# Softmax remainders' products one step later on TensorE, and eleven weight remainders subtracted on VectorE

## The chip, the cores and the metric

One Trainium2 chip, of which the kernel uses one core. A core has TensorE (PE, matrix products into PSUM banks), VectorE (DVE), ScalarE (ACT), GpSimd (POOL) and SyncE (SP), each with its own queue of instructions, which it works off in order, and DMA queues that move data between device memory and SBUF. The metric is the device time of one execution in microseconds. The median of three executions of the kernel before is 932.94 us (932.41 to 934.12).

## The reference

One transformer layer over 128 context tokens and 512 latent tokens of width 1024: RMSNorm with a modulation, one projection into queries, keys and values of two mixers (A: attention with grouped heads; B: attention in a window of the grid with a bias) and into two gates; the gated merge of both mixers, an output projection, and an MLP.

```
aq, ak, av, bq, bk, bv, ga, gb = split(h @ w_in)
p = softmax(scores);  o = p @ v                      # mixer A: 8 heads; mixer B: 8 heads, window + context
m = sigmoid(ga) * (a_o @ w_br_a) + sigmoid(gb) * (b_o @ w_br_b)
x = x + g1 * (m @ w_out)
x = x + g2 * (square(relu(h2 @ w1)) @ w2)
```

Everything is float32.

## The kernel before

A float32 matrix is split into a part that TensorE takes exactly at its fast rate (`hi`, type fp32r) and the remainder `lo = x - hi`. A product is then three: hi by hi, hi by lo, lo by hi (`gemm_k`, L311 to L313). Features lie on the 128 partitions, tokens run along the free axis, in two halves of 320.

**Attention (55 to 322 us).** The sixteen heads run one after another (`HeadA`, `HeadB`, and a `CtxPair` for the context queries after every second head). While one head makes its scores (L674 and L675 in A, L727 and L728 in B) and their exponentials, the head before it is transposed and multiplied with the values, step by step: `T(t)` transposes the probabilities of one key tile on TensorE into a bank `pt` (L684, L744; two such banks), and `p_split` turns it into `ph` (ScalarE, L622) and the remainder `pl` (VectorE, L623). A step later `pv()` multiplies both with the values into the head's bank `po`, of which there is one: L691 and L692 in A (five steps of 512 columns), L755 and L756 in B (four steps with different widths). `pl` is multiplied directly behind `ph` of the same step. At the last step `combine` takes `po` out. `ph`, `pl`, the `ct` of `combine`, the reciprocals `rc` of a pair of heads and the context's `pc` share five tiles of tag `r`. Between these steps stand the projections of later heads and of the gates as filler.

**Merge (322 to 440 us).** For each of eight output tiles n: two gates (tiles 18 + n and 26 + n of `w_in`, 24 products for each half), their sigmoids on ScalarE, then the products of tile n of `w_br` (12 for each mixer and half), multiplied with the gates on VectorE (L1143), added (L1144) and split into `mh` (ScalarE, L1145) and `ml` (VectorE, L1146). Tiles 21, 29, 22 and 30 are made in attention and come back from device memory as `sg`. The weights come in the order 18, 26, `br` 0, 19, 27, `br` 1, 20, 28, `br` 2, `br` 3, `br` 4, 23, 31, `br` 5, and so on. Beside it VectorE makes the modulation for the second half of the layer from 32 transfers (`wmt`, products `mt`, L1065), in portions between the rest.

`Weights.conv()` prepares a weight: it is loaded into `wst` (three tiles), ScalarE makes `hi` (L263), and the remainder is made in one of three ways. For a weight in `LOSET`, which is built from the table `LOACC`, ScalarE writes -hi into `lo` (L265) and GpSimd's queue starts a transfer that reads the weight a second time and adds it (L266). Otherwise VectorE, or for a few weights GpSimd, subtracts (L272, in two halves for `w_in`). `hi` and `lo` have three tiles each, so a weight is converted when the one three places ahead of it is done.

What sets the order: from the merge until the MLP begins, VectorE runs in the order in which the code is written. All other orders of these stages (TensorE, ScalarE, GpSimd, SyncE, and VectorE in attention) are planned when the program is built, from the dependences.

Of the kernel before, what the change touches and what calls it, by code (L numbers as in the profile page):

```python
# [16 lines left out]
P = 128  # L17
# [35 lines left out]
NST = 3  # L53
NB = 4
NU = 6
BLKPOOL = (("A12", "A22"), ())
AUTO = (0, 0)
LAG3 = 5
# [2 lines left out]
TQ = 2  # L61
P3 = 8
GPV = 1
LOACC = (("in", 21, 22), ("in", 29, 30), ("in", 20, 26), ("in", 27, 34), ("br", 0, 8))
FINP = ()
HALVES = (slice(0, HT), slice(HT, NT))

# [2 lines left out]
def trunk_layer(ctx: ExitStack, tc: tile.TileContext, xT, small_in, wmodA, wmodB, tabs, cacheK, cacheV, bias,  # L70
                w_in, w_br, w_out, w1, w2, yT, akT, avT, bkT, bvT):
    nc = tc.nc
    PE, ACT, DVE = nc.tensor, nc.scalar, nc.vector
# [23 lines left out]
    def open_phase(name, nu):  # L97
        phase.close()
        cur["p"] = phase.enter_context(tc.tile_pool(name=name, bufs=1, reuse_waits="tile"))
        cur["nu"] = nu  # L100
        return cur["p"]
# [7 lines left out]
    def o_tile(name, dt=F32):  # L109
        return hp_.tile([P, NT], dt, tag="o", bufs=9, name=name)  # L110
# [4 lines left out]
    def tt_tile(name):  # L115
        return cur["p"].tile([P, NT], F32R, tag="tt", bufs=12, name=name)
# [4 lines left out]
    def ps_(tag, name):  # L121
        return psum["p"].tile([P, 512], F32, tag=tag, bufs=psum["n"][tag], name=name)
# [10 lines left out]
    def ps_t():  # L133
        return ps_("t", "pt")

    def ps_o():
        return ps_("o", "po")

    def r32(ap):
        return ap.bitcast(F32)  # L140
# [162 lines left out]
    EXTRA = {("out", 4), ("w1", 0)}  # L303
    LOSET = {(x, n) for x, a, b in LOACC for n in range(a, b) if x != "in" or n not in GATES[2:]}
    W = Weights()
# [206 lines left out]
    kp = open_phase("attn", 8)  # L512
# [8 lines left out]
    SHUF = [(i + 16) % 32 for i in range(32)]  # L521

    def r_(name, dt=F32):
        return kp.tile([P, 512], dt, tag="r", bufs=5, name=name)

    def rf(name):
        return kp.tile([P, 512], F32, tag="rf", bufs=2, name=name)
# [33 lines left out]
    def half(e):  # L561
        return slice(64 * e, 64 * e + 64)
# [57 lines left out]
    def p_split(pt, n):  # L620
        ph, pl = r_("ph", F32R), r_("pl", F32R)
        ACT.activation(ph[:, :n], pt[:, :n], AF.Copy)  # L622
        DVE.tensor_sub(pl[:, :n], pt[:, :n], r32(ph[:, :n]))  # L623
        return ph, pl

    def combine(dst, ps, n):

        t = r_("ct")
        ACT.activation(t[0:64, :n], ps[64:P], AF.Copy)
        DVE.tensor_add(dst, ps[0:64], t[0:64, :n])  # L630
# [10 lines left out]
    def pair_sums(mixer, j):  # L641
        RC[mixer, j] = r_("rc")
        sm = SUMS[mixer, j]
        DVE.reciprocal(sm, sm)
        ACT.activation(RC[mixer, j].rearrange("p (q e d) -> p q e d", q=4, e=2),
                       sm.rearrange("p (e q) -> p q e", e=2).unsqueeze(3).broadcast_to([P, 4, 2, 64]), AF.Copy)

    def pair_norm(mixer, j):

        rc, o = RC[mixer, j], (AO if mixer == "a" else BO)[j]  # L650
        rows = ps_t()
        for qt in range(4):
            PE.transpose(rows[:, qt * P:(qt + 1) * P], rc[:, qt * P:(qt + 1) * P], ident)
        DVE.tensor_mul(o[:, P:NT], o[:, P:NT], rows)

    class HeadA:
# [24 lines left out]
        def T(self, t):  # L681
            pt = ps_t()
            for qt in range(4):
                PE.transpose(pt[:, qt * P:(qt + 1) * P], self.p[qt][:, t * P:(t + 1) * P], ident)  # L684
            ph, pl = p_split(pt, 512)

            def pv():
                if t == 0:
                    self.po = ps_o()
                v = AV(t + 1, self.g)  # L690
                PE.matmul(self.po, v, ph, start=(t == 0), stop=False)  # L691
                PE.matmul(self.po, v, pl, start=False, stop=(t == 4))  # L692
                if t == 4:
                    combine(AO[self.j][half(self.e), P:NT], self.po, 512)
                    if self.e:
                        after.append(lambda: pair_norm("a", self.j))
                return 470
            if t == 1 and self.e:
                pair_sums("a", self.j)
            return 520, pv  # L700
# [5 lines left out]
    class HeadB:  # L706
# [31 lines left out]
        def T(self, gi):  # L738
            pt = ps_t()
            c = 0  # L740
            for t, q0, q1 in BG[gi]:
                for qt in range(q0, q1):
                    k = (0, 0, 384, 256)[qt] if t == 4 else (P if qt < 2 else 0) + (t - BL[qt]) * P
                    PE.transpose(pt[:, c:c + P], self.p[qt][:, k:k + P], ident)  # L744
                    c += P
            ph, pl = p_split(pt, c)

            def pv():
                if gi == 0:
                    self.po = ps_o()  # L750
                c = 0
                for t, q0, q1 in BG[gi]:
                    n = (q1 - q0) * P
                    v = BV[self.j](5 if t == 4 else t + 1, self.e)
                    PE.matmul(self.po[:, q0 * P:q1 * P], v, ph[:, c:c + n], start=(gi == 0), stop=False)  # L755
                    PE.matmul(self.po[:, q0 * P:q1 * P], v, pl[:, c:c + n], start=False, stop=(gi == 3))  # L756
                    c += n
                if gi == 3:
                    combine(BO[self.j][half(self.e), P:NT], self.po, 512)
                    if self.e:  # L760
                        after.append(lambda: pair_norm("b", self.j))
                return 440
            if gi == 1 and self.e:
                pair_sums("b", self.j)
            return 420, pv
# [262 lines left out]

    open_phase("late", NU)
    v_pool = ExitStack()  # L1030
# [70 lines left out]
    class Units:  # L1101
        n = 0
# [11 lines left out]
    for j in range(4):  # L1114
        for src, dst in ((AO[j], AOS), (BO[j], BOS)):
            d = (tt_tile("osh"), o_tile("osl", F32R))
# [194 lines left out]
    class Operands:  # L1311
# [38 lines left out]
        def conv(self):  # L1350
# [6 lines left out]
            ACT.activation(w[:, 0:4], t, AF.Copy)  # L1357
            (nc.gpsimd if o in BLKPOOL[l - 1] else DVE).tensor_sub(w[:, 4:8], t, r32(w[:, 0:4]))  # L1358
            if o in ("S3", "S2", "A22"):
# [236 lines left out]
    for x in SEQ:  # L1596
        l, c, n, o = x
        w = OPS[0].get(x)
# [143 lines left out]
```

## Time and profile before

| what | value |
|---|---|
| median of three executions | 932.94 us (932.41 to 934.12) |
| the profiled execution | 933.35 us, of which the span is 931.4 us |
| granted TensorE clock | 0.998 |
| transfers | 151.08 MB; q1 (SP) 33.0% of 16 engines' span, q0 (POOL) 29.7% |
| accumulating transfers `wl<-w_in` | 11, of 512 KB, median 8.0 us from issue to landing |
| stage 430 to 525 us, output projection and norm | PE busy 94.88 of 95.00 us, DVE 74.46 |
| stage 525 to 620 us, MLP | PE 95.00 of 95.00 us, DVE 83.45 |

Times are microseconds from the start of the span, unless ns is written. PEld is TensorE's weight load, which runs beside the product ahead of it. L12 is line 12 of the kernel before. A wait of the form "engine line <- engine line" gives its total, how often it occurred, and the longest.

### The profile page before, as it was taken

How to read it: one execution, taken by the hardware profiler on the slowest of the kernel's cores; microseconds unless marked ns; L12 is line 12 of the kernel's file. 1: busy time of each engine (PE TensorE's matmuls, PEld its weight loads, DVE VectorE, ACT ScalarE, POOL GpSimd, SP SyncE). 2: the span in 40 equal slices, each digit the busy share in tenths (PEclk: the TensorE clock that was granted, in tenths of full speed). 3: DMA queues.
4: the chain of work that ended last, by engine and by line, in shares of the span. 5: the costliest groups of instructions: out<-in, count | busy, mean ns of one | idle time of the engine just before them, and what ended most of it. 6: DMA issues, size and time to landing. Idle time of an engine off the chain costs nothing.

```text
span 931.4 us, 16637 instructions
## 1 busy us (share of the span) xinstructions
PE 913.3 (98%) x6166; PEld 879.2 (94%) x6166; DVE 716.2 (77%) x1491; ACT 566.5 (61%) x1153; POOL 193.3 (21%) x223
## 2 busy tenths in 40 slices
PE   9999999999999999999999999999999999999996
PEld 7799889989999999999999999999999999999995
DVE  5665887756756797486688996986798778985898
ACT  4566777756656765765423577536763576457765
POOL 0020200002201011211130010445233532364130
PEclk9999999999999999999999999999999999999999
DMA  9783310125636479999753362888778887798473
GB/s 348 293 241 107 90 44 26 61 67 143 163 87 159 135 240 263 258 237 269 238 160 114 103 192 77 141 191 190 171 128 191 181 170 158 165 191 175 94 114 113
DMA packets 54032, 151.08 MB, mean 162 GB/s; under 512 B 6656, under 2 KB 10384, under 8 KB 53952
## 3 DMA queue, kind: packets, MB, share of 16 engines
q1 hardware_dynamic: 31440, 100.27, 33.0%
q0 software_dynamic: 21360, 48.45, 29.7%
q10 hardware_dynamic: 1152, 1.31, 0.4%
q8 instruction: 48, 0.79, 0.3%
q14 instruction: 32, 0.26, 0.1%
HBM read 138.72 MB, written 4.60 MB: 154 GB/s over the span
## 4 chain that ended last, share of the span: by engine, by line
PE 75%; DVE 8%; issue 6%; DMA 5%; ACT 3%; POOL 1%; SPq 0%; DVEq 0%; POOLq 0%; ACTq 0%
PE b L1611 10%; PE b L1612 10%; PE b L1610 10%; PE pg L311 6%; PE pg L313 6%; PE pg L312 6%; PE pss L313 3%; PE pss L311 3%; PE pss L312 3%; DMA wl<-w_in 2%; PE pt L313 2%; PE pt L311 2%; PE pt L312 2%; PE pt L684 2%; PE pss L402 1%
## 5 line engine op out<-in xcount | busy, mean ns | idle before, releaser
L1357 ACT ACTIVATE wb<-wsb 128x512 fp32r<-128x512 f32 x140 | 87.1, 628 | 93.4 <-PE b L1612 62.1
L1611 PE MATMUL b<-op,wb 128*128 128x320 f32 x448 | 138.8, 310 | 0.7 <-DVE op L1426 0.7
L1610 PE MATMUL b<-op,wb 128*128 128x320 f32 x448 | 138.7, 310 | 0.3 <-ACT op L1425 0.3
L1612 PE MATMUL b<-op,wb 128*128 128x320 f32 x448 | 138.6, 309 | 0.0
L1358 DVE TENSOR_TENSOR wb<-wsb,wb 128x512 fp32r<-128x512 f32 x128 | 94.3, 739 | 28.1 <-ACT wb L1357 27.7
L1361 POOL DMA_DIRECT2D wsb<-w x84 | 73.8, 917 | 128.4 <-DVE wb L1358 92.8
L263 ACT ACTIVATE wh<-wst 128x512 fp32r<-128x512 f32 (+1 forms) x84 | 61.0, 739 | 41.2 <-PE pg L312 19.0
L1065 DVE SCALAR_TENSOR_TENSOR mt<-wmt,cb 128x512 f32<-128x512 f32 x128 | 80.9, 687 | 5.8 <-DMA wmt<-wmodB 5.6
L1611 PEld LDWEIGHTS b<-op,wb 128*128 128x128 f32 x448 | 84.2, 188 | 1.2 <-DVE op L1426 1.2
L1610 PEld LDWEIGHTS b<-op,wb 128*128 128x128 f32 x448 | 84.2, 188 | 0.8 <-ACT op L1425 0.5
L1612 PEld LDWEIGHTS b<-op,wb 128*128 128x128 f32 x448 | 84.1, 188 | 0.0
L623 DVE TENSOR_TENSOR pl<-pt,ph 128x512 fp32r<-128x512 f32 (+2 forms) x80 | 50.6, 634 | 21.0 <-ACT ph L622 17.3
L1342 POOL DMA_DIRECT2D wsb<-w x28 | 26.6, 949 | 138.5 <-DMA wsb<-w 45.1
L622 ACT ACTIVATE ph<-pt 128x512 fp32r<-128x512 f32 (+2 forms) x80 | 43.9, 552 | 17.4 <-PE pt L744 7.8
L272 DVE TENSOR_TENSOR wl<-wst,wh 128x512 fp32r<-128x512 f32 (+1 forms) x51 | 40.4, 802 | 16.9 <-ACT wh L263 16.4
L1469 DVE SCALAR_TENSOR_TENSOR x<-b,parts,x 128x128 f32<-128x128 f32 (+1 forms) x116 | 46.5, 430 | 2.7 <-PE b L1612 1.7
L1610 PE MATMUL b<-t,wb 128*128 128x320 f32 x144 | 44.6, 310 | 0.4 <-DVE tp L1455 0.4
L1611 PE MATMUL b<-t,wb 128*128 128x320 f32 x144 | 44.5, 309 | 0.0
L1612 PE MATMUL b<-t,wb 128*128 128x320 f32 x144 | 44.5, 309 | 0.0
L1357 ACT ACTIVATE wb<-wst 128x512 fp32r<-128x512 f32 x56 | 34.7, 625 | 16.1 <-PE b L1612 9.2
L1426 DVE TENSOR_TENSOR op<-hid,op 128x1280 fp32r<-128x1280 f32 (+2 forms) x32 | 37.0, 1155 | 7.8 <-ACT op L1425 7.8
L1469 DVE SCALAR_TENSOR_TENSOR x<-tp,parts,x 128x320 f32<-128x320 f32 (+2 forms) x60 | 39.8, 691 | 1.0 <-ACT tp L1514 1.0
(874 smaller groups left out, 3019.9 us busy)
## 6 DMA issues: line engine op xcount, KB each, us to landing
wsb<-w POOLq DMA_DIRECT2D x112, 256.0 KB, 5.2
wst<-w SPq DMA_DIRECT2D x36, 512.0 KB, 4.2
wmt<-wmodB SPq DMA_DIRECT2D x32, 512.0 KB, 5.3
wst<-w_in SPq DMA_DIRECT2D x31, 512.0 KB, 4.3
wsb<-w SPq DMA_DIRECT2D x28, 512.0 KB, 4.2
ms<-wmodA SPq DMA_DIRECT2D x16, 512.0 KB, 7.8
wl<-w_in POOLq DMA_DIRECT2D x11, 512.0 KB, 8.0
bt<-bias SPq DMA_DIRECT2D x16, 320.0 KB, 5.3
```

Source lines behind the costliest of these rows:

```text
L263: ACT.activation(hi[:, ks], st[:, ks], AF.Copy)
L311: PE.matmul(ps, wh[:, k], xh[:, sl], start=first, stop=False)
L312: PE.matmul(ps, wh[:, k], xl[:, sl], start=False, stop=False)
L313: PE.matmul(ps, wl[:, k], xh[:, sl], start=False, stop=last)
L1065: DVE.scalar_tensor_tensor(t, st[:, q * 512:(q + 1) * 512], 1.0, r32(cb[2 * q + i][:, :512]), op0=OP.mult, op1=OP.mult, accum_out=parts[:, ...
L1357: ACT.activation(w[:, 0:4], t, AF.Copy)
L1358: (nc.gpsimd if o in BLKPOOL[l - 1] else DVE).tensor_sub(w[:, 4:8], t, r32(w[:, 0:4]))
L1361: nc.gpsimd.dma_start(t, self.src(l, c, n, e)[:, 4 * half:4 * half + 4], accum_op=OP.add)
L1469: DVE.scalar_tensor_tensor(X1[i][:, sl], src[:, sl.start - off:sl.stop - off], g[:, j:j + 1], X1[i][:, sl], op0=OP.mult, op1=OP.add)
L1610: PE.matmul(b, w[:, k], xh, start=not whole and k == 0, stop=False, skip_group_check=True)
L1611: PE.matmul(b, w[:, k], xl, start=False, stop=False, skip_group_check=True)
L1612: PE.matmul(b, w[:, 4 + k], xh, start=False, stop=o not in ("A11", "S2", "S1") and k == 3, skip_group_check=True)
```

## The change

Two things. The product with the remainder `pl` moves one step back in `pv()`: a step multiplies its own `ph` and then the `pl` of the step before; the last step does both that are left. And the table `LOACC` gets smaller: tiles 20, 27 and 28 of `w_in` and all eight of `w_br` leave it, so that these eleven remainders are subtracted on VectorE (L272); tiles 21, 29, 23, 24, 25, 31, 32 and 33 stay. The number of `r` tiles gets a name and stays five.

```diff
+NR = 5
-LOACC = (("in", 21, 22), ("in", 29, 30), ("in", 20, 26), ("in", 27, 34), ("br", 0, 8))
+LOACC = (("in", 21, 22), ("in", 29, 30), ("in", 22, 26), ("in", 30, 34))
...
                 if t == 0:
                     self.po = ps_o()
+                    self.late = []
                 v = AV(t + 1, self.g)
                 PE.matmul(self.po, v, ph, start=(t == 0), stop=False)
-                PE.matmul(self.po, v, pl, start=False, stop=(t == 4))
+                self.late.append((v, pl))
+                while self.late and (t == 4 or len(self.late) > 1):
+                    w, q = self.late.pop(0)
+                    PE.matmul(self.po, w, q, start=False, stop=(t == 4 and not self.late))
...
                     PE.matmul(self.po[:, q0 * P:q1 * P], v, ph[:, c:c + n], start=(gi == 0), stop=False)
-                    PE.matmul(self.po[:, q0 * P:q1 * P], v, pl[:, c:c + n], start=False, stop=(gi == 3))
+                    self.late.append((gi, self.po[:, q0 * P:q1 * P], v, pl[:, c:c + n]))
                     c += n
+                while self.late and (gi == 3 or self.late[0][0] < gi):
+                    _, d, w, q = self.late.pop(0)
+                    PE.matmul(d, w, q, start=False, stop=(gi == 3 and not self.late))
```

In the changed kernel the lines are numbered one to nine higher: L691 and L692 are L693 and L697, L755 and L756 are L761 and L766, L272 is L273, L1065 is L1074.

TensorE in an early head of mixer A, before the change, with what each row waits for: the `pl` of step 0 (1017), filler, the transposes of step 2, and the `ph` of step 1.

```order
L692 MATMUL po_1049<-pl_1017,vst_764 128x512 [waits DVE_49]
L311 MATMUL pg_1061<-h1h_307,wh_797 128x320
L312 MATMUL pg_1061<-h1l_308,wh_797 128x320
L313 MATMUL pg_1061<-h1h_307,wl_798 128x320
L311 MATMUL pg_1061<-h2h_360,wh_797 128x320
L312 MATMUL pg_1061<-h2l_361,wh_797 128x320
L313 MATMUL pg_1061<-h2h_360,wl_798 128x320
L684 MATMUL pt_1071<-pk_74,pa_903 128x128 [waits PE_49]
L684 MATMUL pt_1071<-pk_74,pa_926 128x128
L684 MATMUL pt_1071<-pk_74,pa_944 128x128
L684 MATMUL pt_1071<-pk_74,pa_965 128x128
L691 MATMUL po_1049<-ph_1045,vst_764 128x512 [waits Activation_49]
```

The same place after it, from the transposes of step 2 on (L685), with the `ph` of step 1 (L693) and the `pl` of step 0 (L697).

```order
L685 MATMUL pt_1070<-pk_74,pa_903 128x128 [waits DVE_49,PE_49]
L685 MATMUL pt_1070<-pk_74,pa_926 128x128
L685 MATMUL pt_1070<-pk_74,pa_944 128x128
L685 MATMUL pt_1070<-pk_74,pa_965 128x128
L693 MATMUL po_1049<-ph_1045,vst_764 128x512 [waits Activation_49]
L697 MATMUL po_1049<-pl_1017,vst_764 128x512
L675 MATMUL pss_1081<-kh_721,qs_730 128x320 [waits PE_49,Activation_49]
L676 MATMUL pss_1081<-kl_722,qs_730 128x320
```

The product with `pl` 1017 has moved behind `ph` 1045 and waits for nothing of its own; the wait for VectorE now stands at the transposes, six rows behind where it stood. Over the whole kernel 31 of 40 rows of L692 wait before and 6 of 40 after, of L756 28 and 8.

VectorE in the merge before the change, where the products of `br` 0 for the first half are gated (L1143); `mt` is the modulation.

```order
L1065 SCALAR_TENSOR_TENSOR mt_4175,parts_3974<-wmt_4173,cb_4040 128x512
L1065 SCALAR_TENSOR_TENSOR mt_4177,parts_3974<-wmt_4173,cb_4041 128x512
L1143 TENSOR_TENSOR sg_4036<-pss_4187,sg_4036 128x320
L1143 TENSOR_TENSOR sg_4130<-pt_4201,sg_4130 128x320
L1144 TENSOR_TENSOR sg_4036<-sg_4036,sg_4130 128x320
L1146 TENSOR_TENSOR ml_4010<-sg_4036,mh_4009 128x320
L1065 SCALAR_TENSOR_TENSOR mt_4218,parts_3974<-wmt_4173,cb_4042 128x512
```

And after it (L1152 is L1143, L1155 is L1146).

```order
L1074 SCALAR_TENSOR_TENSOR mt_4174,parts_3973<-wmt_4172,cb_4039 128x512
L1074 SCALAR_TENSOR_TENSOR mt_4176,parts_3973<-wmt_4172,cb_4040 128x512
L273 TENSOR_TENSOR wl_4181<-wst_3694,wh_4180 128x512 x2
L1152 TENSOR_TENSOR sg_4035<-pss_4186,sg_4035 128x320
L1152 TENSOR_TENSOR sg_4129<-pt_4200,sg_4129 128x320
L1153 TENSOR_TENSOR sg_4035<-sg_4035,sg_4129 128x320
L1155 TENSOR_TENSOR ml_4009<-sg_4035,mh_4008 128x320
```

The two halves of the remainder of tile 27 (`wl_4181`) now stand ahead of the gating; before, GpSimd's queue made it.

ScalarE at the same time before the change: `mh` is the split of the first and second half of output tile 0, `wh_4342` and `wl_4343` are tile 20, and `sg_4373` is the sigmoid of the first half of tile 27.

```order
L1145 ACTIVATE mh_4009<-sg_4036 128x320
L263 ACTIVATE wh_4342<-wst_4179 128x512
L1096 ACTIVATE sg_4326<-pss_4301 128x320
L263 ACTIVATE wh_4342<-wst_4179 128x512
L1097 ACTIVATE sg_4326<-sg_4326 128x320
L265 ACTIVATE wl_4343<-wh_4342 128x1024
L1145 ACTIVATE mh_4009<-sg_4083 128x320
L1098 ACTIVATE sg_4326<-sg_4326 128x320
L1096 ACTIVATE sg_4373<-pg_4348 128x320
L1097 ACTIVATE sg_4373<-sg_4373 128x320
```

And after it (L1154 is L1145, L264 is L263, L1105 to L1107 are L1096 to L1098).

```order
L264 ACTIVATE wh_4340<-wst_4178 128x512
L1154 ACTIVATE mh_4008<-sg_4035 128x320
L1105 ACTIVATE sg_4324<-pss_4299 128x320
L264 ACTIVATE wh_4340<-wst_4178 128x512
L1106 ACTIVATE sg_4324<-sg_4324 128x320
L1107 ACTIVATE sg_4324<-sg_4324 128x320
L1105 ACTIVATE sg_4371<-pg_4346 128x320
L1106 ACTIVATE sg_4371<-sg_4371 128x320
L1154 ACTIVATE mh_4008<-sg_4082 128x320
```

The copy into `wl` is gone; the first `mh` has moved behind the first half of tile 20, and the second `mh` behind the first two steps of the sigmoid of tile 27.

More of the change, by code (lines that the diff above doesn't have):

```diff
@@ L523, in r_ @@
     def r_(name, dt=F32):
-        return kp.tile([P, 512], dt, tag="r", bufs=5, name=name)
+        return kp.tile([P, 512], dt, tag="r", bufs=NR, name=name)
     def rf(name):
@@ L750, in pv @@
                     self.po = ps_o()
+                    self.late = []
                 c = 0
```

## The prediction

> **What bounds the kernel now.** I read the page first, then the busy time by stage, then who waited for whom on the weight loads of TensorE, then the timeline at the places that these waits name.
>
> ```profile
> span 931.4 us, 16637 instructions
> PE 913.3 (98%) x6166; PEld 879.2 (94%) x6166; DVE 716.2 (77%) x1491; ACT 566.5 (61%) x1153; POOL 193.3 (21%) x223
> PE 75%; DVE 8%; issue 6%; DMA 5%; ACT 3%; POOL 1%; SPq 0%; DVEq 0%; POOLq 0%; ACTq 0%
> ```
>
> TensorE is busy 98% of the span and is three quarters of the chain that ended last. VectorE's 77% and ScalarE's 61% cost something only where TensorE stands for them. So the question is how long TensorE stands in the two stages that the change touches.
>
> ```profile
> 55.00:216.00 161.00, 157.53 (x1025) 145.62 (x1024) 117.02 (x216) 110.28 (x252) 16.06 (x22) 1.00 0.31 90
> 216.00:322.00 106.00, 105.34 (x710) 99.19 (x709) 70.41 (x184) 69.19 (x172) 14.31 (x27) 1.00 0.49 130
> 345.00:430.00 85.00, 84.88 (x579) 84.62 (x578) 60.48 (x186) 53.55 (x105) 14.35 (x20) 1.00 0.95 269
> ```
>
> Columns: stretch, length, then busy time of TensorE, its weight loads, VectorE, ScalarE and GpSimd, the granted clock, the DMA share and GB/s. In mixer A (first row) TensorE's matmuls leave 3.5 us open, in mixer B 0.7 us, in the middle of the merge 0.1 us. Weight loads are open for longer (15.4 and 6.8 us), and they show the stalls better, since a matmul that is held up is still drawn as running. The DMA engines are 95% busy in the merge.
>
> **Part one: the remainder's product one step later (L691/L692 and L755/L756).** No matmul is added or removed. All that can go is time in which TensorE stood for `pl`.
>
> ```profile
> PEld po L691 <- ACT ph L622: 3.6, 5, 1.2
> PEld po L692 <- DVE pl L623: 1.9, 7, 0.7
> PEld pt L684 <- DVE pl L623: 1.3, 3, 0.5
> PEld po L691 <- DVE ao L630: 0.8, 3, 0.3
> PEld po L756 <- DVE nm L733: 0.5, 3, 0.2
> ```
>
> These are waits between 55 and 322 us (total, times, longest). For `pl`, TensorE waited 1.9 us at L692 in seven places and 0.5 us at L756 in three (VectorE is named with `nm`, its last instruction before `pl`). That is 2.4 us, not the 80 products times some price. Is there also a price for every wait, even one that is met long before? The built order takes the wait off 25 rows of L692 and 20 of L756, so 0.09 us each would be a lot. A stretch of mixer B answers it:
>
> ```profile
> 291.33 0.49 PE L744 MATMUL pt<-pk,pb 128*128 128x128 f32 x3
> 291.57 0.36 PE L755 MATMUL po<-ph,vst 128*128 128x256 f32 x1
> 291.77 0.28 PE L756 MATMUL po<-pl,vst 128*128 128x256 f32 x1
> 291.89 0.28 PE L755 MATMUL po<-ph,vst 128*128 128x256 f32 x1
> 292.01 0.28 PE L756 MATMUL po<-pl,vst 128*128 128x256 f32 x1
> 292.13 0.31 PE L311 MATMUL pg<-h4h,wh 128*128 128x320 f32 x1
> ```
>
> From L755 to L756 it takes 0.20 us the first time and 0.12 us the second, at the same size. The first pair stands behind transposes and its rows wait; the second does neither. Which of the two costs the 0.08 us? Mixer A has an L692 that waits in the order but stands behind a product of the gates:
>
> ```profile
> 100.72 0.30 PE L313 MATMUL pg<-h7h,wl 128*128 128x320 f32 x1
> 100.86 0.39 PE L692 MATMUL po<-pl,vst 128*128 128x512 f32 x1
> 101.09 0.60 PE L684 MATMUL pt<-pk,pa 128*128 128x128 f32 x4
> ```
>
> It starts 0.14 us after L313, the usual step between products of 320 columns, and the transposes follow 0.23 us later: a wait that is already met costs nothing. So the 0.08 us belongs to the first long product behind transposes, and there is as much of that after the change as before. The Trainium skill, TensorE: Matmul & The Clock Gate, section Architectural detail: the array is 16× 32×32, not 1× 128×128, says that TensorE's queue can pull weight loads ahead of matmuls in flight; read as a rule for this change, it would pay for each wait taken away, since a held load can't be pulled ahead. The same page, section Back-to-back issue gap, says that a matmul of 128 columns is spaced by its weight load too (about 81 ns); the row at 291.33 agrees, with three of them in 0.24 us. By the first the sum would be some 4 us lower, by the second as I make it; the L692 at 100.86 speaks for the second.
>
> Nor does the wait vanish: as the order shows, it moves from L692 to the next transposes into the same `pt` bank, which need `pl` to have been read out of it. At the place shown with the change that is six rows later, six products of some 0.15 us, 0.9 us; the longest wait of L692 is 0.7 us, so that lead covers it. The last remainder of a head keeps its wait (6 and 8 rows), with one more product ahead of it.
>
> From 2.4 us I take the 0.09 us of the weight load in each of ten places: 1.5 us. Not all of this reaches the end. What is late next is `ph`: 3.6 us in five places, where ScalarE sets the pace, and TensorE only gets there sooner. The order is also planned anew over the whole of attention, and some first products now come earlier, ahead of the `ao` that they wait for. I take half, **0.8 us**; the bounds are 2.4 us gained and, with `ao` and `ph` waits grown by half (2.2 us of 4.4), 2.2 us lost.
>
> **Part two: eleven remainders on VectorE in place of transfers.** Where did TensorE stand in the merge?
>
> ```profile
> PEld pg L313 <- DMA wl<-w_in: 2.1, 1, 2.1
> PEld pt L313 <- DMA wl<-w_in: 0.4, 1, 0.4
> PEld pss L313 <- DVE wl L272: 0.4, 1, 0.4
> ...
> 341.56 0.31 PE L312 MATMUL pg<-h0l,wh 128*128 128x320 f32 x1
> 343.75 0.41 PE L313 MATMUL pg<-h0h,wl 128*128 128x320 f32 x1 [1.88 <-DMA wl<-w_in]
> 344.00 0.30 PE L311 MATMUL pg<-h1h,wh 128*128 128x320 f32 x1
> ...
> 333.72 0.89 POOL L266 DMA_DIRECT2D wl<-w_in  x1 [10.64 <-ACT wl L265]
> DMA to landing us min/median/max: 10.0/10.0/10.0
> ```
>
> The large stall is at tile 27, the second gate of the second output tile. Its accumulating transfer is issued at 333.72 and lands 10.0 us later; the product that needs it would have started at 341.71. After the change it is this remainder that VectorE makes. When?
>
> ```profile
> L272 DVE TENSOR_TENSOR wl<-wst,wh x51: 669/692/1227, 50.9 to 552.3; 128x512 fp32r<-128x512 f32 x40, 128x1024 fp32r<-128x1024 f32 x11
> L265 ACT ACTIVATE wl<-wh x19: 1042/1048/1062, 43.3 to 436.6; 128x1024 fp32r<-128x1024 f32 x19
> 333.72 1.29 DVE L272 TENSOR_TENSOR wl<-wst,wh 128x512 fp32r<-128x512 f32 x2
> 338.60 0.49 DVE L1143 TENSOR_TENSOR sg<-pss,sg 128x320 f32<-128x320 f32 x1
> ...
> 347.27 0.44 ACT L1096 ACTIVATE sg<-pg 128x320 f32<-128x320 f32 x1 [2.31 <-PE pg L313]
> ...
> 350.89 0.31 PE L313 MATMUL pt<-osh,wl 128*128 128x320 f32 x1
> ```
>
> In the new order the subtraction stands right before the L1143 that began at 338.60. Two halves take 1.29 us, so it is done at 339.9, 1.8 us before TensorE wants it. That gives **2.1 us**. The tightest of the others is `br` 1. Its subtraction stands behind the second `ml`, which needs the second `mh`, and this now stands in ScalarE's order behind the sigmoid of tile 27's first half. That sigmoid began at 347.27 and comes 2.1 us earlier with the stall gone, 345.2. Three ScalarE steps of 0.45 us, as this row has them, and `ml`, as large as L1143, 0.49, make 347.0, the subtraction 1.2 more, 348.2. TensorE wants it at 350.89 less 2.1, 348.8: some 0.5 us to spare. Of the two stalls of 0.4 us, one is a transfer that stays and one is already VectorE's; I leave both.
>
> The eleven subtractions cost VectorE six halves of 0.69 and eight wholes of 1.23 us, 14 us; ScalarE loses eleven copies of 1.05 us, GpSimd eleven issues. Is there room on VectorE?
>
> ```profile
> 322.00:342.00 20.00, 18.70 (x45) 1.00 0.70 203
> 342.00:372.00 30.00, 24.02 (x73) 1.00 0.97 284
> 372.00:402.00 30.00, 16.08 (x46) 1.00 0.89 235
> ```
>
> VectorE alone: idle 1.3, 6.0 and 13.9 us. Three remainders of `w_in` (27, 20, 28) and two of `br` (1, 2) take 6.6 us of the 7.3 idle up to 372, so it runs full there and gets its slack back by 402. Behind a late subtraction stand the modulation products and L1143, which frees the banks of TensorE; seven banks of at least 1.8 us of product each (twelve of 0.15) are more lead than the few microseconds by which VectorE can fall behind. If that cover were gone, the price would be the lag itself, which is the third rival. Bounds for this part: 0 to 2.9 us gained (2.1 and both of 0.4).
>
> **The sum.** The profiled execution took 933.35 us (span 931.4 and 1.95 around it), 0.4 above the median of 932.94. 933.35 - 2.1 - 0.8 = 930.45, and by the median 930.0. I say **930.4**.
>
> **Rivals.**
> First: attention keeps what it has, since ScalarE's `ph` sets the pace there, and only tile 27's stall goes: 933.35 - 2.1 = 931.2. For it speaks that the longest waits are for `ph`.
> Second: each wait taken away pays 0.09 us: 45 of them are 4.05, with 2.1 in the merge 927.2. The row at 100.86 speaks against it.
> Third: the remainder is as late from VectorE as it was by transfer, at `br` 1 or behind it: 933.35 - 0.8 = 932.5. VectorE's order is fixed by hand, and the margin is 0.5 us.
> Fourth, the other side: the five `r` tiles.
>
> ```profile
> ACT rc L645 <- PE po L691: 1.1, 2, 0.7
> DVE pl L623 <- PE po L691: 2.1, 1, 2.1
> ```
>
> `ph`, `pl`, `ct` and `rc` share them, and `rc` holds one for most of every second head. Such waits exist already. Now `pl` is held a step longer, so ScalarE's and VectorE's next tile waits for a product of TensorE more often, and TensorE then waits for `ph`. If each of the eight heads with an `rc` pays one 0.7 us on TensorE, that is 5.6: 933.35 - 2.1 + 5.6 = 936.9. It decides as soon as ScalarE gets its tile later than `ph` is needed, which is so already in five places.
>
> **Chances and range.** The forecast 0.48 (its own range 929.2 to 931.4), first rival 0.16, second 0.08, third 0.16, fourth 0.12. The range 927.9 to 932.8 leaves out the second and the fourth, which are 0.2. A measurement of this kernel tells some 0.2% from no change, 1.9 us: faster is below 931.1. The forecast is there in 0.41 of its 0.48, the first rival in 0.07 of 0.16, the second wholly: 0.56. Slower is the fourth and a little of the third: 0.13. Same is the rest: 0.31.
>
> **What the profile after would show.** The wait of the weight load of `pg` L313 for `wl<-w_in` of 2.1 us is gone, and no wait of L313 for VectorE above 0.5 us is in its place. The seven waits of L692 for `pl` shrink to at most three, L756 likewise. The step from an L755 of 256 columns behind transposes to its follower stays at 0.20 us; if it falls to 0.12, the second rival is right. A wait for `ph` of more than 5 us between 55 and 322 us, or new ScalarE waits for `po`, would show the first or the fourth. I am wrong if the merge gives nothing, or if attention moves by more than 2.4 us either way.

## The result, and the profile after

The changed kernel takes **934.62 us** (median of 22 executions, 930.58 to 937.97) against 932.70 for the kernel before (22 executions beside them): a ratio of 1.0025, 95% interval 1.0017 to 1.0034. It is slower by a quarter of a per cent (a second set of twelve executions, `after_b` below, gives 1.0013 and does not tell it from no change); forecast was 930.4, faster. The profiled execution took 934.50 us, its span 932.7, so 1.3 us more span than before.

Three lines of the page of the changed kernel:

```profile
span 932.7 us, 16635 instructions
PE 913.2 (98%) x6166; PEld 880.2 (94%) x6166; DVE 727.8 (78%) x1505; ACT 555.5 (60%) x1142; POOL 183.3 (20%) x212
PE 81%; DVE 8%; issue 4%; ACT 3%; DMA 3%; POOL 1%; SPq 0%; DVEq 0%; ACTq 0%; POOLq 0%
```

TensorE's busy time is the same to 0.1 us. VectorE has 11.6 us more, ScalarE 11.0 us less and GpSimd 10 us less; VectorE's remainders alone went from 40.4 us to 54.3. The sums by stage, with the columns of the prediction's table:

```profile
55.00:216.00 161.00, 157.45 (x1033) 146.68 (x1031) 117.97 (x219) 111.35 (x255) 16.05 (x22) 1.00 0.31 91
216.00:322.00 106.00, 105.87 (x719) 100.38 (x717) 72.25 (x186) 69.24 (x171) 14.36 (x27) 1.00 0.45 124
345.00:430.00 85.00, 81.99 (x547) 81.47 (x546) 66.00 (x183) 45.93 (x95) 8.74 (x13) 0.98 0.68 200
```

In attention TensorE gets a little further in the same time: in the 106 us of mixer B it starts 719 matmuls in place of 710. In the merge, where before it stood for 0.1 us of 85, it now stands for 3.0, and the granted clock is 0.98. The DMA engines, 95% busy there before, are at 68%, so over the stage as a whole the loss is not one of bandwidth.

To see where time was won and lost I matched the matmul rows of both timelines by line and operands and took the difference of their start times. Each column is a place in the program, by the time at which TensorE passed it before (65 us: early in attention; 328: the merge begins; 352: behind tile 27; 392: tile 23; 447: the merge ends), the last is the difference of the spans. Minus is earlier than before. The experiments below are in the same table.

| kernel | 65 | 328 | 352 | 392 | 447 | end |
|---|---|---|---|---|---|---|
| changed kernel | +0.1 | -2.3 | -4.4 | -4.4 | +0.3 | +1.3 |
| the same again | +0.2 | -2.2 | -4.3 | -4.3 | +0.8 | +2.0 |
| late_only | -0.6 | -2.3 | -3.7 | -3.7 | -2.3 | -1.5 |
| acc_only | 0.0 | 0.0 | -2.1 | -2.1 | +6.3 | +5.7 |
| only27 | -0.2 | -1.9 | -4.1 | -4.1 | -3.0 | -4.2 |
| br_dma | +0.1 | -0.7 | -2.8 | -2.8 | -1.2 | +0.6 |
| br_pool | +0.8 | -0.8 | -2.9 | -2.9 | +2.9 | +2.2 |
| pace | -0.2 | -2.1 | -4.1 | -4.1 | -4.5 | +9.8 |
| no31 | +0.3 | -1.6 | -3.7 | -3.7 | +1.5 | +2.8 |
| no31_24 (second) | +0.5 | -1.4 | -3.5 | -3.5 | -3.9 | -4.5 |
| acc_no31_24 | +0.1 | 0.0 | -2.0 | -2.0 | -2.4 | -3.4 |
| all_dve | +0.3 | -1.6 | -3.7 | -3.7 | -4.1 | -5.7 |

The changed kernel is 4.4 us ahead at tile 23, more than the 2.9 forecast, and **loses 4.7 us between there and the end of the merge**. The waits of its weight loads from 55 to 460 us name the places:

```profile
PEld po L693 <- ACT ph L623: 4.0, 7, 1.2
PEld pt L314 <- DMA wl<-w_in: 2.1, 1, 2.1
PEld pg L314 <- DMA wl<-w_in: 1.4, 1, 1.4
...
PEld pt L685 <- DVE pl L624: 0.8, 2, 0.4
...
PEld po L697 <- DVE pl L624: 0.5, 1, 0.5
```

The stall at tile 27 is gone. Two others have come, at tiles 31 (1.4 us) and 24 (2.1 us), both for adding transfers that the change left as they were. The windows around them in the changed kernel (length, TensorE, weight loads, VectorE, ScalarE, GpSimd, clock, DMA share, GB/s):

```profile
396.00:398.00 2.00, 0.93 (x6) 0.93 (x7) 0.99 (x3) 1.97 (x5) 0.00 (x0) 1.00 0.04 8
398.00:402.00 4.00, 4.00 (x29) 4.00 (x28) 3.43 (x9) 2.19 (x6) 0.00 (x0) 1.00 0.00 0
...
412.00:414.00 2.00, 0.72 (x5) 0.72 (x6) 1.32 (x5) 0.00 (x0) 0.00 (x0) 1.00 1.06 324
414.00:416.00 2.00, 2.00 (x10) 2.00 (x10) 1.90 (x10) 0.00 (x0) 0.00 (x0) 0.55 1.05 266
416.00:418.00 2.00, 2.00 (x10) 2.00 (x9) 1.43 (x4) 0.69 (x2) 0.00 (x0) 0.60 1.03 375
418.00:420.00 2.00, 2.00 (x16) 2.00 (x15) 1.60 (x4) 1.07 (x2) 0.00 (x0) 1.00 0.89 358
```

Two things are to be seen. Behind the stall at tile 24 the clock falls to half for some 3.4 us (0.55 and 0.60 as means of two windows of 2 us): ten products in 2 us where there are sixteen or so, which costs another 1.6 us (tile 24 takes 8.2 us from its first product with `wl`, where others take 6.6). And from 396 to 402 us the DMA engines are idle (0.04 and 0.00): in this time the transfer for tile 24 was not slow, it was not there yet. It is issued at 404.02 and then does meet full engines (1.03 from 408 to 412 us), but the 9.2 us to its landing are no more than the 10.0 us that it took before the change.

Why were they issued late? The chain at tile 31, from the timeline of the changed kernel, all engines, in order of time:

```profile
374.68 1.23 DVE L273 TENSOR_TENSOR wl<-wst,wh 128x1024 fp32r<-128x1024 f32 x1
375.82 0.49 DVE L1152 TENSOR_TENSOR sg<-pg,sg 128x320 f32<-128x320 f32 x1
...
376.96 0.90 POOL L267 DMA_DIRECT2D wl<-w_in  x1 [13.85 <-ACT wl L266]
377.53 1.57 POOL L1138 DMA_DIRECT2D sg<-gate  x2
...
385.49 0.47 ACT L1105 ACTIVATE sg<-sg 128x320 f32<-128x320 f32 x1 [5.39 <-DMA sg<-gate]
...
389.21 1.04 ACT L266 ACTIVATE wl<-wh 128x1024 fp32r<-128x1024 f32 x1
...
390.65 0.92 POOL L267 DMA_DIRECT2D wl<-w_in  x1
...
395.62 0.31 PE L313 MATMUL pg<-h0l,wh 128*128 128x320 f32 x1
397.07 0.41 PE L314 MATMUL pg<-h0h,wl 128*128 128x320 f32 x1 [1.14 <-DMA wl<-w_in]
```

Read it from the top. VectorE gates the first bank of `br` 2 at 375.82, directly behind a remainder. TensorE had begun `br` 2 at 367.32, so the gating is 8.5 us behind that. Before, the same row stood 2.0 us behind (373.74 against 371.71) and VectorE was waiting for TensorE. The gates of the later tiles that come back from device memory (`sg<-gate`) need tiles that the gating frees, so GpSimd's queue issues the next of them only at 377.53, 1.7 us behind the gating. By then the adding transfer of tile 23 stands ahead of it in the same queue (376.96, landing 8.1 us later), and the reload lands right behind that one. This is the reload that ScalarE waits for; its row alone gives who waited, and its time to landing:

```profile
  ACT sg L1105: 5.4, 1
DMA to landing us min/median/max: 7.9/7.9/7.9
```

ScalarE, in order, stands 5.39 us for it, and behind it in ScalarE's queue stands the copy of -hi for tile 31, without which its adding transfer can't start. How much of the 5.39 us is the late gating and how much the transfer ahead, `all_dve` shows below: there the gating is as late, no transfer stands ahead, and ScalarE waits 0.8 us.

The two rows of the kernel before that answer to it:

```profile
373.74 0.49 DVE L1143 TENSOR_TENSOR sg<-pg,sg 128x320 f32<-128x320 f32 x1 [1.00 <-PE pg L313]
...
391.90 0.89 POOL L266 DMA_DIRECT2D wl<-w_in  x1 [2.52 <-ACT wl L265]
```

This allows two theories. **A**: TensorE is simply 4.4 us earlier, and adding transfers that stay are paced by ScalarE and do not come earlier (390.65 against 391.90 at tile 31). **B**: the added remainders overbook VectorE from 345 to 380 us and hold the transfers back through the chain above. (**C**, for the attention part only: the earlier start of the merge is chance in one profile.)

### The profile page after: what moved, and what is told of

It reads as the page before. It is cut to its first block, busy times and chain, and to the rows that moved or that the text cites. A ratio compares the mean times of both kernels' runs of the same rounds, so it can differ in the third digit from the quotient of the medians.

```text
span 932.7 us, 16635 instructions
## 1 busy us (share of the span) xinstructions
PE 913.2 (98%) x6166; PEld 880.2 (94%) x6166; DVE 727.8 (78%) x1505; ACT 555.5 (60%) x1142; POOL 183.3 (20%) x212
## 4 chain that ended last, share of the span: by engine, by line
PE 81%; DVE 8%; issue 4%; ACT 3%; DMA 3%; POOL 1%; SPq 0%; DVEq 0%; ACTq 0%; POOLq 0%
PE b L1620 9%; PE b L1619 9%; PE b L1621 9%; PE pg L312 7%; PE pg L313 7%; PE pg L314 7%; PE pss L314 3%; PE pss L313 3%; PE pss L312 3%; PE pt L314 2%; PE pt L313 2%; PE pt L312 2%; PE pt L685 2%; PE pss L403 1%; PE pt L749 1%
## 5 line engine op out<-in xcount | busy, mean ns | idle before, releaser
L264 ACT ACTIVATE wh<-wst 128x512 fp32r<-128x512 f32 (+1 forms) x84 | 61.2, 739 | 44.2 <-PE pg L313 17.6
L1074 DVE SCALAR_TENSOR_TENSOR mt<-wmt,cb 128x512 f32<-128x512 f32 x128 | 80.8, 688 | 4.1 <-DMA wmt<-wmodB 4.1
L273 DVE TENSOR_TENSOR wl<-wst,wh 128x512 fp32r<-128x512 f32 (+1 forms) x65 | 54.3, 844 | 17.2 <-ACT wh L264 16.9
L623 ACT ACTIVATE ph<-pt 128x512 fp32r<-128x512 f32 (+2 forms) x80 | 44.0, 551 | 15.9 <-PE po L693 3.9
```

Of the source, the lines that this page charges most:

```text
L264: ACT.activation(hi[:, ks], st[:, ks], AF.Copy)
L1074: DVE.scalar_tensor_tensor(t, st[:, q * 512:(q + 1) * 512], 1.0, r32(cb[2 * q + i][:, :512]), op0=OP.mult, op1=OP.mult, accum_out=parts[:, ...
```

## The experiments

Ratios are to the kernel before, run on the same chip beside them, with their 95% intervals.

### One half of the change each

`late_only`: the changed kernel with the old table.

```diff
-LOACC = (("in", 21, 22), ("in", 29, 30), ("in", 22, 26), ("in", 30, 34))
+LOACC = (("in", 21, 22), ("in", 29, 30), ("in", 20, 26), ("in", 27, 34), ("br", 0, 8))
```

> Only the product with pl moves; all transfers stay as before. Theory A (TensorE comes earlier, the adding transfers do not, so they are late): attention gives 2.3 us up to tile 18, as in the changed kernel, but the transfer of tile 27 then meets a TensorE that is up to 2.3 us earlier, its stall of 2.1 us grows to between 2.1 and 4.4: 930.4 to 932.7 us. Theory B (the remainders added to VectorE hold the later transfers up): nothing is added here, the stall at tile 27 stays 2.1 us: 930.4 us. Theory C (the gain up to tile 18 is noise of one profile): 932.7 us and no earlier start of tile 18.

Measured: 931.54 us, ratio 0.9997 (0.9981 to 1.0013). The merge starts 2.3 us earlier, as in the changed kernel. The stall at tile 27 was 0.8 us here, less than either theory said; smaller ones followed:

```profile
PEld pg L314 <- DMA wl<-w_in: 1.2, 2, 0.8
PEld pt L314 <- DMA wl<-w_in: 0.7, 1, 0.7
PEld pss L314 <- DMA wl<-w_in: 0.7, 1, 0.7
```

Together they are 2.6 us, against 2.5 us for adding transfers before, and at 447 us the kernel is still 2.3 us ahead. So C falls, and TensorE's earlier arrival by itself does not make the transfers later; A is weakened. At the end 1.5 us are left in the profile, and the timed runs can't tell that from nothing.

`acc_only`: the kernel before with the new table, the old order of `pl`.

```diff
-LOACC = (("in", 21, 22), ("in", 29, 30), ("in", 20, 26), ("in", 27, 34), ("br", 0, 8))
+LOACC = (("in", 21, 22), ("in", 29, 30), ("in", 22, 26), ("in", 30, 34))
```

> Only the eleven remainders move to VectorE; attention as before. A: the stall of 2.1 us at tile 27 goes, TensorE is 2.1 us earlier instead of 4.4, so the stalls at tiles 31 and 24 shrink to about 0 and 1 us and no half clock follows: 931 to 932 us. B: VectorE is as loaded as in the changed kernel, the copies for 31 and 24 are as late as there against TensorE, stalls of 3.3 us and perhaps the half clock of 1.6: 933.9 to 935.5 us.

Measured: 935.24 us, ratio 1.0035 (1.002 to 1.005), as B has it. Its waits in the merge and the two issues on GpSimd's queue, for tiles 31 and 24:

```profile
PEld pt L313 <- DMA wl<-w_in: 2.8, 1, 2.8
PEld pg L313 <- DMA wl<-w_in: 2.7, 1, 2.7
```

```profile
394.03 0.93 POOL L266 DMA_DIRECT2D wl<-w_in  x1
408.18 0.87 POOL L266 DMA_DIRECT2D wl<-w_in  x1 [13.23 <-ACT wl L265]
```

Attention is the old one, the merge begins when it did before, and TensorE is only 2.1 us ahead at 392 us. Yet the stalls are larger than in the changed kernel, and the issues at 394.03 and 408.18 are 2.1 and 3.7 us **later than before by the clock** (391.90 and 404.49), the second in part since TensorE had stood in between. The first A can't make. (The profile is of the slowest of its twelve executions, 938.91 us, so the stalls may be larger in it than in most.) The half of the change that was to gain most is the half that loses.

### Taking the late transfers away, and the load away

`no31_24`: the two transfers that are late become remainders on VectorE as well, which has then still more to do. It ran twice; the profile is of the second.

```diff
-LOACC = (("in", 21, 22), ("in", 29, 30), ("in", 22, 26), ("in", 30, 34))
+LOACC = (("in", 21, 22), ("in", 29, 30), ("in", 22, 24), ("in", 25, 26), ("in", 32, 34))
```

> The changed kernel with the remainders of tiles 31 and 24 on VectorE too. A: the stalls of 1.4 and 1.9 us and the half clock of 1.6 us behind them go: 934.6 - 4.9 = 929.7 us, up to 931 if tile 32 or 25 is late next. B: VectorE gets 2.6 us more, its remainders of 31 and 24 are as late as the transfers were: 934 us or more, with waits of L314 for VectorE in place of those for a transfer.

> The changed kernel with tiles 31 and 24 on VectorE too, once more, for a profile. B: the gates' reload stays as late as in the changed kernel and ScalarE waits there, but no transfer hangs on it: no wait of L314 for a transfer at 31 and 24, no half clock, 930.5 us again. If VectorE itself makes 31 late, a wait for VectorE of over 1 us stands there.

Measured: 930.65 us, ratio 0.9974 (0.996 to 0.9988), and 928.59 us, ratio 0.9959 (0.9945 to 0.9973). TensorE does not stand in the merge any more, and the clock stays full:

```profile
372.00:402.00 30.00, 30.00 (x207) 30.00 (x206) 20.31 (x55) 16.77 (x39) 4.15 (x7) 1.00 0.57 174
402.00:430.00 28.00, 28.00 (x193) 28.00 (x193) 23.92 (x72) 16.28 (x34) 2.61 (x3) 1.00 0.79 237
```

ScalarE still stands for the reload (5.3 us at its longest), but nothing that TensorE needs soon hangs on it. VectorE's own remainders are in time in spite of the 2.6 us added. So VectorE's lateness costs nothing by itself; it costs through the adding transfers behind it.

`only27`: the changed kernel, but of the eleven remainders only that of tile 27 goes to VectorE.

```diff
-LOACC = (("in", 21, 22), ("in", 29, 30), ("in", 22, 26), ("in", 30, 34))
+LOACC = (("in", 21, 22), ("in", 29, 30), ("in", 20, 26), ("in", 28, 34), ("br", 0, 8))
```

> The product with pl moves and only tile 27 of the weights goes to VectorE (1.3 us of work); 20, 28 and br stay adding transfers. A: TensorE is 4.4 us earlier and the transfers that stay are late against it, at 20, 28, 31 or 24, 2 us or more: 930.5 to 933 us. B: VectorE is hardly more loaded than before, no stall follows: 928.3 us.

Measured: 930.39 us, ratio 0.9983 (0.9967 to 0.9999). One stall of 1.5 us at tile 24, none at 31: between B's 928.3 and A's 930.5 to 933, at A's end. TensorE is as early here as in the changed kernel, so A has a share of the stall at 24; the rest of it, and all of that at 31, goes with the other ten remainders on VectorE.

`pace`: the converse. Transfers and remainders as in the changed kernel, but the code that sets modulation products between the merge's steps is told of the remainders' time.

```diff
-                mod_pace(650)
+                mod_pace(650 if 18 + 8 * i + n not in (20, 27, 28) else 1950)
...
-            mod_pace(2600 if n < KT - 1 else 5000)
+            mod_pace(3220 if n < KT - 1 else 5000)
```

> The changed kernel with fewer modulation products set between the merge's steps on VectorE: the planned room is cut by what the eleven remainders take (13.8 us), and these products follow later, in the output projection. Transfers as in the changed kernel. Theory B (VectorE is overbooked from 345 to 380 us, its gating is late, with it the reload of the gates in GpSimd's queue, ScalarE stands behind that reload, and the copies for the transfers of tiles 31 and 24 stand behind ScalarE): the stalls of 1.4 and 1.9 us and the half clock go, 934.6 - 4.9 = 929.7 us, up to 931. Theory A (TensorE is simply too early for the transfers that stay): stalls as in the changed kernel, 934.6 us.

Measured: 943.01 us, ratio 1.0109 (1.0093 to 1.0125). As a total the expectation failed by far. In the merge it held exactly: no stall, TensorE 4.5 us ahead at its end, the best of all kernels there. VectorE gates the same bank of `br` 2 at 369.86, 2.3 us behind the 367.57 at which TensorE began it, and waits for TensorE at the next; the transfer for tile 31 is issued at 385.79, 4.9 us earlier than in the changed kernel, at the same place of TensorE to 0.3 us:

```profile
369.86 0.48 DVE L1152 TENSOR_TENSOR sg<-pg,sg 128x320 f32<-128x320 f32 x1
371.29 0.49 DVE L1152 TENSOR_TENSOR sg<-pss,sg 128x320 f32<-128x320 f32 x1 [0.95 <-PE pss L314]
...
385.79 0.89 POOL L267 DMA_DIRECT2D wl<-w_in  x1 [3.02 <-ACT wl L266]
```

From 370 to 380 us VectorE is busy 3.98 us before, 8.98 in the changed kernel and 5.07 here (the same window of each, VectorE alone):

```profile
370.00:380.00 10.00, 3.98 (x11) 1.00 1.00 315
```

```profile
370.00:380.00 10.00, 8.98 (x24) 1.00 0.93 294
```

```profile
370.00:380.00 10.00, 5.07 (x11) 1.00 0.59 173
```

What it loses, it loses later. The modulation is needed at the norm behind the output projection, and what had not been done by then comes in one piece. The chain of work that ended last, and the wait behind it:

```profile
513.64 1.99 DVE mt L1074 x8
...
519.90 0.79 ACT hh6h L338 x2
520.74 0.64 PE pss L312
```

```profile
PEld pss L312 <- ACT hh6h L338: 5.8, 1, 5.8
```

This wait is less than half of the 14.3 us that `pace` loses behind the merge. The clock is at half behind it for 6.8 us (0.55, 0.50, 0.50 and 0.75 in the windows of 2 us from 520 to 528 us), and near 638 and 645 us TensorE stands for VectorE twice more, 1.4 and 2.2 us, with half clock behind again (0.62 and 0.53 from 646 to 650).

So the load on VectorE is shown as the cause, and this way of removing it is not a cure: what is put off is missing at the norm. What `pace` does not part is VectorE's lag from the order that is planned with it: in its GpSimd queue the reload stands ahead of tile 23's transfer (372.60 against 377.89) and lands in 3.0 us. It also puts off loads, which empties the DMA engines (0.59 against 0.93 in the windows above).

How late a transfer is, is its lead: from its issue (the row of GpSimd's queue) to the product that needs it (0.29 us behind the first product of the tile, as two products are).

| kernel | tile 31: issue, needed, lead, stall | tile 24: issue, needed, lead, stall |
|---|---|---|
| before | 391.9, 400.2, 8.3, none | 404.5, 414.2, 9.7, 0.4 |
| acc_only | 394.0, 398.6, 4.5, 2.7 | 408.2, 415.3, 7.1, 2.8 |
| changed | 390.7, 395.8, 5.1, 1.4 | 404.0, 411.3, 7.2, 2.1 |
| only27 | 388.0, 396.1, 8.1, none | 401.2, 410.2, 8.9, 1.5 |
| pace | 385.8, 396.0, 10.2, none | 398.9, 410.1, 11.2, none |

The stall (by the rows of waits) follows the lead: in the kernels of the table that stall, the transfer of 31 lands 6.4 to 7.1 us after its issue, that of 24 9.2 to 10.3. Before the change they took 6.6 and 10.0, so it is the lead that has changed and not the transfer; and `pace` has more lead than any landing at these tiles took in these runs (7.8 and 10.4).

### Which part of the load, and other ways of carrying it

`br_dma`: the changed kernel with `("br", 0, 8)` back in the table. `br_pool`: the changed kernel with these eight remainders on GpSimd.

```diff
-    WPOOLSET = {("out", n) for n in range(WPO, KT)} | {("w1", n) for n in range(WP1)}
+    WPOOLSET = {("br", n) for n in range(KT)} | {("out", n) for n in range(WPO, KT)} | {("w1", n) for n in range(WP1)}
```

> The changed kernel with the eight w_br remainders back as adding transfers; 20, 27 and 28 stay on VectorE (3.9 us). B: VectorE is not overbooked after 360 us, no stall at 31, at most 1.5 us at 24 as with only tile 27 moved: 930 to 931 us. If the remainders of 20 and 28 are enough to make VectorE late: about 934 us.

> The changed kernel with the eight w_br remainders subtracted on GpSimd (8 x 2.41 us) in place of VectorE; neither transfers nor VectorE have them. B: no stall at 31, at most 1.5 us at 24: 929.5 to 931 us, unless GpSimd holds up its own queue of reloads (then about 934). A: 934.6 us as the changed kernel.

Measured: `br_dma` 932.80 us, ratio 1.0006 (0.999 to 1.0022), with one stall of 1.8 us, at tile 23 and not at 24; `br_pool` 936.43 us, ratio 1.0039 (1.0027 to 1.0052), with a stall of 3.9 us at tile 23. Both fell short of B's numbers: the first has less gain than expected, the second none. In `br_dma` the remainders of tiles 20 and 28 are load enough: `only27` differs from it in these two alone, gates `br` 2 3.0 us behind TensorE in place of 7.1, and issues the transfer for tile 23 at 381.17 in place of 384.90. There the lead is 5.4 us, and the transfer lands in 7.1. For `br_pool` the reason stands in VectorE's groups from 345 to 392 us, in the changed kernel and here:

```profile
L1074 DVE SCALAR_TENSOR_TENSOR mt<-wmt,cb 128x512 f32<-128x512 f32 x32 | 20.0, 688 | 0.0
```

```profile
L1074 DVE SCALAR_TENSOR_TENSOR mt<-wmt,cb 128x512 f32<-128x512 f32 x33 | 27.3, 886 | 0.0
```

The mean of a modulation product is 886 ns in place of 688, but this is no slowing of all of them. Thirty take 0.68 or 0.69 us, and three, those that begin while GpSimd subtracts, take 2.89, 2.94 and 2.90 us and end some 0.55 us behind the subtraction. The first of the three, with its subtraction:

```profile
356.02 2.78 POOL L270 TENSOR_TENSOR wl<-wst,wh 128x1024 fp32r<-128x1024 f32 x1 [18.80 <-ACT wh L264]
356.46 2.89 DVE L1074 SCALAR_TENSOR_TENSOR mt<-wmt,cb 128x512 f32<-128x512 f32 x1
```

VectorE stands until GpSimd is done: 6.7 us for the three, while four remainders, 4.9 us by the 1.22 us of one, were taken from it in that time. It is later than before the relief (11.0 us behind TensorE at `br` 2 in place of 8.5). The Trainium skill, SBUF — State Buffer, section Who interferes with whom, says that a VectorE instruction with two inputs from SBUF contends with GpSimd instructions that read SBUF; the trace agrees, with these three products.

### How much further

`no31`: only tile 31 more on VectorE. `acc_no31_24`: the kernel before with the table of `no31_24`, so without the move of `pl`. `all_dve`: every remainder of the merge on VectorE. `after_b`: the changed kernel once more. The tables:

```diff
+LOACC = (("in", 21, 22), ("in", 29, 30), ("in", 22, 26), ("in", 32, 34))
...
+LOACC = (("in", 21, 22), ("in", 29, 30), ("in", 22, 24), ("in", 25, 26), ("in", 32, 34))
...
+LOACC = (("in", 21, 22), ("in", 29, 30))
```

> The changed kernel once more, beside the others on one chip: 0.25% over the kernel before, stalls of L314 for the transfers of 31 and 24 of 1 to 3 us each at 395 to 414 us; whether half clock follows them depends on the run.

> The changed kernel with tile 31 alone on VectorE; 24 stays an adding transfer. Theory B: no stall at 31; the one at 24 stays at 1.5 to 2.5 us, since ScalarE's copy for it still stands behind its wait for VectorE: between the changed kernel and the one without both, 930.5 to 932.5 us. If the stall at 31 was the cause of the one at 24, no stall is left: 929 us.

> Without the move of pl: the old attention, with 20, 27, 28, w_br, 31 and 24 on VectorE. B: the merge runs without a stall as with pl moved; the merge starts 1.6 us later (327.3 us against a mean of 325.7 in seven profiles with pl moved), so this is 1.6 us, 0.17%, slower than the same with pl moved: 930.5 us. If the move of pl is worth nothing at the end, they are alike: 929 us.

> The changed kernel with every remainder of the merge on VectorE (23, 24, 25, 31, 32 and 33 too; 8 us more than in the changed kernel, only 21 and 29 stay transfers). B: no transfer is left to be late; VectorE is later still with its gating, so either no stall (929 us, as without 31 and 24), or TensorE waits for remainders from VectorE, over 1 us, in 390 to 440 us, and modulation is pushed into the output projection: 931 us or more.

Measured: `after_b` 933.17 us, ratio 1.0013 (0.9996 to 1.0031), stalls of 0.7 us at 31 and 3.3 us at 24 and half clock behind the second; by these executions alone it can't be told from the kernel before. `no31` 933.41 us, ratio 1.0011 (0.9997 to 1.0026): no stall at 31, 3.5 us at 24, so the stall at 24 has its own cause and does not go with the one ahead of it (in two profiles of the changed kernel it is 2.1 and 3.3 us). `acc_no31_24` 930.01 us, ratio 0.9978 (0.9967 to 0.999): no stall in the merge; the move of `pl` is worth 1.5 us there at 447 us (-2.4 against -3.9), and the timed intervals overlap. `all_dve` **928.57 us, ratio 0.9956 (0.994 to 0.9973)**: no stall, though VectorE is nearly full:

```profile
402.00:430.00 28.00, 28.00 (x193) 28.00 (x192) 26.64 (x81) 11.58 (x24) 0.00 (x0) 1.00 0.69 217
```

In `all_dve` the gating of `br` 2 is late by the same 8.5 us as in the changed kernel, and the reload is issued as far behind it (1.7 us, at 378.21). But no adding transfer stands ahead in GpSimd's queue: the reload lands in 3.3 us in place of 7.9, and ScalarE waits 0.8 us for it in place of 5.4. So of that wait 4.6 us are tile 23's transfer, one of those that stayed.

`no31_24` and `all_dve` beat both kernels; between the two the intervals don't decide.

## Why the prediction was wrong

**The move of `pl`: right mechanism, too small.** I took 0.8 us. Between the places 65 and 328 of the table the changed kernel gains 2.4 us, and the ten profiles with the move gain 0.8 to 2.4, on the mean 1.8; the two without it gain 0.1 each. (The 0.8 is `br_dma`, where TensorE ran at half clock for 3.4 us from 132.5 us on; the others gain 1.6 or more.) What goes is what the prediction named: waits for `pl` (L692, L756 and L684 before; L697 and L685 after), 3.7 us before and 1.3 in the rows above (0.3 more at L654), while waits for `ph` grew from 3.6 to 4.0. I halved the gain for that and needn't have. Nor does any row show the 0.09 us that I took off in each of ten places: the steps at 291.33 show 0.08, and a weight load of 128 columns takes 0.19. One wait that I had not counted grew: at 132 us TensorE stands 1.2 us (`pg` L312, named with `po` L697) where it stood 0.4 before. The second rival falls by its own test, the step behind transposes. For 256 columns it is 0.20 us at all seven places of the changed kernel, as forecast; for 384 columns this is one:

```profile
290.83 0.49 PE L749 MATMUL pt<-pk,pb 128*128 128x128 f32 x3
291.07 0.42 PE L761 MATMUL po<-ph,vst 128*128 128x384 f32 x1
291.33 0.40 PE L766 MATMUL po<-pl,vst 128*128 128x256 f32 x2
```

From L761 to L766 it is 0.26 us for 384 columns, 0.18 by the rate of the 320-column products, so still 0.08 more, though L766 waits for nothing here. The reordering of weight loads that I cited from the Trainium skill (TensorE: Matmul & The Clock Gate) brought nothing for a wait taken away, and 45 removed waits at 0.09 would have been 4.05 us. The fourth rival, the `r` tiles, did not cost either. ScalarE now does wait with `ph` for products that free a tile, which it never did before; two rows of what it waited for at L623 (total, times):

```profile
  PE po L693: 3.9, 4
  PE po L761: 3.6, 3
```

But TensorE's own waits for `ph` grew by 0.4 us only.

**Tile 27: right.** 2.1 us were forecast, 2.1 were gained (-2.3 to -4.4). The remainder of `br` 1 was done at 345.84, needed at 346.49: a margin of 0.65 us, forecast 0.5. The third rival did not come true where it was placed. One reading was wrong: of the two stalls of 0.4 us that I put into the merge, the one for VectorE's remainder (`pss` L313) stands at 520.6 us, behind the output projection, and it is there after the change too.

**VectorE's lag: this is the step that failed.** I wrote that VectorE "runs full there and gets its slack back by 402", and that behind it stood only the modulation products and the gating, "which frees the banks of TensorE; seven banks [...] are more lead than the few microseconds by which VectorE can fall behind". The lag was 6.5 us at `br` 2 (8.5 behind TensorE in place of 2.0), and the banks did hold: no wait of TensorE for a gating stands in the changed kernel's list (they only just held: `acc_only` and `no31` have one each, of 0.5 and 0.6 us). But banks are not all that the gating frees. It also frees the `sg` tiles, into which GpSimd's queue reloads the gates; the late reload lands behind tile 23's adding transfer, ScalarE stands for it, and the copies for the next adding transfers stand behind that. I listed who waits for TensorE's banks and not who else waits for the same instruction. I followed the eleven weights that were moved and set the eight that stayed at nothing ("one is a transfer that stays [...] I leave both"), although one of them, tile 24, was already 0.4 us late. `acc_only` shows the loss without the other half of the change, `pace` shows it gone without the load, `no31_24` without the transfers.

**The clock** was in no term of the sum. After the stall at tile 24 it cost 1.6 us, a third of what the merge lost.

The sum with the measured terms: -2.4 in attention and 0.1 ahead of it, -2.1 at tile 27, +4.7 for tiles 31 and 24 and the clock, +1.0 behind the merge: +1.3, the difference of the spans. The last term is open: between 447 us and the end the kernels drift by -1.6 to +1.8 us against the kernel before (`pace` apart), with no edit there. From 447 to 640 us each keeps its place to 0.1 us; the drift lies behind that, in the MLP. It goes with no part of the change that I could find, and a single profile is uncertain by that much.

## What to carry to other kernels

Before work is moved onto an engine that has to run in order, list everything that its late instructions release, not only the banks of the bottleneck: tiles that a reload waits for, what stands ahead of that reload in its own queue, and whatever stands behind it in another in-order queue. Then give each transfer that stays its lead, from issue to need, and compare it with its time to landing; a lead that only just suffices is the next stall, and when TensorE comes earlier or the issuing queue later it opens. Here moving all remainders (0.9956) was better than moving eleven of them (1.0025 and 1.0013), which was no better than moving none.

## What the runs showed of the hardware

A stall of TensorE can cost twice. After five of the seven stalls of 2.0 us or more in the merges of these kernels (2.1, 2.8, 3.3, 3.5 and 3.9 us) products went at about half rate for a while, 0.27 us each in place of 0.146, which cost 1.6 us four times and 2.9 once; after the other two (2.1 us before, at tile 27, and 2.7 us in `acc_only`) and after ten shorter ones, of 0.4 to 1.8 us, they did not. The Trainium skill, TensorE: Matmul & The Clock Gate, section What's actually happening, describes a gate that halves the clock after an idle window of about 3.4 us, where the windows run on by themselves. The half rate and its length agree (3.4 us after four of the five, 6.8 after the stall of 2.8 us in `acc_only`); but 2.1 us of standing were enough, and that equal stalls went one way and the other fits windows that are not tied to the program. So does a place in attention: from 130 to 132 us TensorE is busy 0.81 of 2.00 us in `br_dma` and 0.82 in the changed kernel, and the half clock follows in the first alone. It may also spread the times: 7.4 us lie between the fastest and the slowest of 22 executions of the changed kernel (the three fastest have a mean clock of 0.997 and 0.998, the three slowest of 0.992 to 0.994), 3.8 us of the kernel before.

The second is the price of GpSimd's help: while it subtracted 128x1024 (2.41 to 2.78 us), a VectorE product that began beside it stood until it was done, 2.9 us in place of 0.69, so that relieving VectorE of 4.9 us cost it 6.7.

The third is that GpSimd's DMA queue delivered in order: in the merges of 13 traces none of 207 transfers landed before the one ahead of it in that queue. A reload of 160 KB lands 2.4 us after its issue at best; behind an adding transfer of 512 KB that was still under way it took 4.3 to 10.8 us.
